# A hybrid SSD and attention block: the attention stage's banks, order and score pipeline rearranged

## The chip, the core and the metric

The kernel runs on one core of one Trainium2 chip. Its time is in device microseconds (us), taken over repeated executions; the profile shows one execution. The engines are TensorE (PE, with its weight loads as PEld), VectorE (DVE), ScalarE (ACT), GpSimd (POOL) and SyncE (SP, which here only starts transfers). Each takes its instructions in the order in which they were written into its queue, and waits where an operand or a buffer is not ready.

## The reference

One layer for 512 tokens of width 2048, float32. An input projection makes everything that two mixers need; an SSD (state space) mixer and an attention mixer give 1024 columns each; an output projection, a norm and a gated feed-forward stage follow.

```python
u = rmsnorm(h, attn_norm_w[l])
z, xbc, dt_raw, q, kc, vc, ks, vs, kw, vw, gate_raw = jnp.split(u @ w_in[l], split_at, axis=-1)
y_ssd = ssd_mixer(z, xbc, dt_raw, ...)       # ends in rmsnorm(y * silu(z), norm_w)
y_att = nsa_mixer(q, kc, vc, ks, vs, kw, vw, gate_raw, ...)
h = h + jnp.concatenate([y_ssd, y_att], axis=-1) @ w_out[l]
v = rmsnorm(h, ffn_norm_w[l])
h = h + (jax.nn.silu(v @ w_gate[l]) * (v @ w_up[l])) @ w_down[l]
return rmsnorm(h, final_norm_w)
```

The attention mixer has 16 heads in four groups of four; a group shares keys and values. Each head has three branches that are added under gates: 31 compressed keys (made from `kc` and `vc` by a small two-layer network), selected blocks of keys (with 512 tokens all eight blocks are selected, so this is causal attention over `ks`, `vs`), and a window of 512 (causal attention over `kw`, `vw`). Queries and keys of the last two are rotated (rope).

## The kernel before, in words

Every float32 product is made of three products of "high" and "low" parts: high by high, high by low, low by high. ACT copies a tile to make its high part (`a_hi`, L118), DVE subtracts to make the low part (`lo`, L121). So every weight tile passes ACT and DVE before PE can use it.

The input projection is cut into 41 **units**. A unit loads 128 output columns of `w_in` in four pieces (`wraw`), splits them (`whi`, `wlo`) and runs 16 k-steps of three matmuls of 512 columns (L241 to L243, in `run_unit`), 48 in all, into one PSUM bank. In order: dt and gates, the SSD inputs, four KC units (the inputs of the compression), Z0 to Z3, and then, group by group, [Z4, Z5 before group 1, Z6 before group 2, Z7 before group 3,] VS, KS, Q0, Q1. After them 16 half units, OS0 to OS15 (24 matmuls each), multiply the SSD half of `w_out`; and 16 more, which the text calls OA, its attention half (L1252 to L1254), with the weight blocks of the later stages. From the seventh unit on all units take turns in two banks, `ps_g`. The other six banks belong to chains: `ps_s` (two: scores), `ps_t` (two: transposes), `ps_v` (products with values), `ps_m` (everything small).

What becomes of a unit's result is its **chain**, a Python generator (`ev_vs`, `ev_ks`, `ev_q`, `ev_z`, `ev_os`, ...). Each `yield n` lets n steps pass. The small class `Sched` holds all chains; `tick` advances them by one step. `run_unit` calls `tick` after every k-step, so that the instructions of the chains are written between the weight matmuls. Where something must be finished first, `run_until` ticks without writing weight matmuls: for a unit, when the chain of the unit but one before has ended (the flag `evac`, set at the end of the whole chain); at `pre_att`, when the compression is done and the pools of the SSD stage can be closed for those of attention; and at others that `wait` for flags.

Chains hold each other up by named holds and single buffers: `ro` (rope's result; a K or Q chain holds it to its end), `qv`, `m` (bank `ps_m`), `fo`. Values are transposed through `ps_m` (L713), keys and queries get rope (two small transfers through POOL's queue, one product on DVE, one on POOL).

The chain `attention` is one generator for all groups. For each group it waits for K, V and both Q of that group, then makes the softmax over the compressed keys (`sc`), transposes it (L864), and only then runs 32 items (four heads, two branches, four query blocks), a new one every second step, through stages: scores on PE (L883, L884), maximum on DVE (L893), exponential on ACT (L900), norm on DVE or ACT (L906, L908), transpose on PE (L926), high part on ACT and low part `ptl` on DVE, and, after a branch's fourth block, eight products with the values on PE (L949). A group's pipeline is run empty before the next group begins.

From VS0 on, each `run_unit` stands under `tc.manual_schedule()`: its instructions are queued as the program wrote them. Elsewhere the library's scheduler is free to reorder instructions between writing and queueing, by its own estimate of their times.

The sum of squares for the SSD norm is kept in `acc2`; its statistics (`rms_stats`, matmuls L292, transposes L302) are made at the beginning of OS0's chain. `ms_hook` loads the eight finished SSD tiles during the last unit of the projection and splits them on ACT and DVE. `stat_s` makes the statistics of the next norm after OS15.

Of the kernel before, what the change touches and what calls it, by code (L numbers as in the profile page):

```python
# [27 lines left out]
EB = 5  # L28
# [80 lines left out]
def body(ctx, tc, xT, w_in, w_out, w_gate, w_up, w_down, w1k, w1v, cols, rows, kst, out):  # L109
# [111 lines left out]

    def run_unit(u):
# [8 lines left out]
        p = p[:, 0:u.cols[1] - u.cols[0]]  # L231
        for i, k0, n in u.sub:
# [89 lines left out]
    def ev_dtg(p):  # L322
# [3 lines left out]
        mul(dve, t, p[0:64, :], rrow[0:64, :])  # L326
        yield 2
# [46 lines left out]
    def conv(t, p):  # L374

        sp = pools["ssd"][1]
        xp = sp.tile([128, 515], F32, tag="xpad", name="xpad", bufs=2)
        dve.memset(xp[:, 0:3], 0.0)
        mul(dve, xp[:, 3:515], p, rrow)
        y = sp.tile([128, 512], F32, tag="c", name="cv", bufs=3)  # L380
# [179 lines left out]
    def ev_z(t):  # L560
        def ev(p):
            yield from sch.wait("r1", ("y", t // 4))
            g, j = divmod(t, 4)
            if g == 0:
                sp = pools["ssd"][1]
                zs = sp.tile([128, 512], F32, tag="zs", name="zs", bufs=2)
                mul(dve, zs, p, rrow)
                act.activation(zs, zs, AF.Silu)
# [4 lines left out]
            else:  # L573
# [6 lines left out]
                mul(dve, zs, p, rrow)  # L580
                yield 1
# [16 lines left out]
    def ev_kc(g):  # L598
        def ev(p):
# [5 lines left out]
            for n, b in (("kc2", 0), ("vc2", 64)):  # L605
                for par in range(2):
                    mul(dve, R[n][par * 64:par * 64 + 64, g, :], p[b:b + 64, par::2], rrow[b:b + 64, par::2])
            if g == 3:
# [92 lines left out]
    def ev_vs(g):  # L701
        def ev(p):
# [4 lines left out]
            mul(dve, t, p, rrow)  # L707
            yield 2
# [39 lines left out]
    def ev_ks(g):  # L748
        def ev(p):
# [4 lines left out]
            mul(dve, t, p, rrow)  # L754
            yield 1
# [32 lines left out]
    def ev_q(g, j):  # L788
        def ev(p):
# [4 lines left out]
            mul(dve, t, p, rrow)  # L794
            yield 1
# [32 lines left out]

    def attention():
        yield from sch.wait("att", "cmp")  # L830
        ap = pools["att"][1]
        vpad = ap.tile([128, 4, 128], F32R, name="vpad")
# [3 lines left out]
        for g in range(4):  # L836
            yield from sch.wait(("k", g), ("v", g), ("q", g, 0), ("q", g, 1))
            kh, kl = R["k", g]
            v = R["v", g]

            sc = R["sc", g]
            sm = ap.tile([128, 3, 4, 4], F32, tag="sm", name="sm", bufs=1)
            dve.tensor_reduce(sm[:, 0], sc, AX.X, ALU.max)
            dve.tensor_scalar(sm[:, 0], sm[:, 0], -1e20, None, op0=ALU.max)
            dve.tensor_tensor(sc.rearrange("p i h k -> p (i h) k"), sc.rearrange("p i h k -> p (i h) k"),
                              sm[:, 0].rearrange("p i h -> p (i h)")[:, :, None].to_broadcast([128, 16, 32]),
                              ALU.subtract)
            yield 1
            act.activation(sc, sc, AF.Exp, scale=0.125)
            for h in range(4):  # L850
                a_hi(vpad[32 * h:32 * h + 32, h, 0:64], vcmp[:, g, :])
            yield 2
            for h in range(4):
                lo(dve, vpad[32 * h:32 * h + 32, h, 64:128], vcmp[:, g, :], vpad[32 * h:32 * h + 32, h, 0:64])
            dve.tensor_reduce(sm[:, 1], sc, AX.X, ALU.add)
            dve.tensor_scalar(sm[:, 1], sm[:, 1], 1e-30, None, op0=ALU.max)
            dve.reciprocal(sm[:, 2], sm[:, 1])
            mul(dve, sm[:, 2], sm[:, 2], gat[:, :, 12 * g:12 * g + 12:3])
            mul(dve, sc.rearrange("p i h k -> p (i h) k"), sc.rearrange("p i h k -> p (i h) k"),
                sm[:, 2].rearrange("p i h -> p (i h)")[:, :, None].to_broadcast([128, 16, 32]))  # L860
            yield 6
            p = ps_t()
            for i in range(4):
                pe.transpose(p[:, i * 128:(i + 1) * 128], sc[:, i].rearrange("p h k -> p (h k)"), ident)  # L864
            sch.flags.add(("sc", g))
            yield 1
            ch = ap.tile([128, 512], F32R, tag="cph", name="cph", bufs=1)
            cl = ap.tile([128, 512], F32R, tag="cpl", name="cpl", bufs=1)
            a_hi(ch, p)
            yield 1  # L870
            lo(dve, cl, p, ch)
            yield 2

            items = [(h, br, i) for h in range(4) for br in range(2) for i in range(4)]
            pt, pr, po = {}, {}, {}

            def score(h, br, i):
                L = 128 * (i + 1)  # L880
                q = R["rq", g, h // 2][:, h % 2, i * 128:(i + 1) * 128]
                p = pr[h, br, i] = ps_s()
                pe.matmul(p[:, 0:L], q, kh[:, br, 0:L], start=True, stop=False)  # L883
                pe.matmul(p[:, 0:L], q, kl[:, br, 0:L], start=False, stop=True)  # L884
                if (br, i) == (1, 3):
                    sch.flags.add(("h", g, h))

            def top(h, br, i):
                L = 128 * (i + 1)
                p = pr[h, br, i]  # L890
                e = ap.tile([128, 512], F32, tag="e", name="e", bufs=EB)
                m = ap.tile([128, 4], F32, tag="em", name="em", bufs=EB + 1)
                dve.tensor_tensor_reduce(e[:, 0:L], p[:, 0:L], kcs(K_AM + 512 - L, L), -0.125, 3e38,  # L893
                                         ALU.add, ALU.min, m[:, 0:1])
                pr[h, br, i] = (e, m)

            def expo(h, br, i):
                L = 128 * (i + 1)
                e, m = pr[h, br, i]
                act.activation(e[:, 0:L], e[:, 0:L], AF.Exp, scale=-1.0, bias=m[:, 0:1], accum_out=m[:, 1:2])  # L900

            def norm(h, br, i):
                L = 128 * (i + 1)
                e, m = pr[h, br, i]
                gc = (4 * g + h) * 3 + 1 + br
                dve.reciprocal(m[:, 2:3], m[:, 1:2])  # L906
                if br:
                    dve.tensor_scalar(e[:, 0:L], e[:, 0:L], m[:, 2:3], gat[:, i, gc:gc + 1],  # L908
                                       op0=ALU.mult, op1=ALU.mult)
                else:  # L910
                    mul(dve, m[:, 3:4], m[:, 2:3], gat[:, i, gc:gc + 1])

            def norm2(h, br, i):
                L = 128 * (i + 1)
                e, m = pr[h, br, i]
                if not br:
                    a_hi(e[:, 0:L], e[:, 0:L], scale=m[:, 3:4])

            def trans(h, br, i):
                e, m = pr[h, br, i]  # L920
                if i == 0:
                    pt[h, br] = (ap.tile([128, 13, 128], F32R, tag="pth", name="pth", bufs=2),
                                 ap.tile([128, 13, 128], F32R, tag="ptl", name="ptl", bufs=2))
                p = ps_t()
                for kb in range(i + 1):
# [963 lines left out]
```

## Time and profile before

| | |
|---|---|
| median of 3 runs | 2312.17 us (2308.17 to 2313.32) |
| span of the profiled execution | 2311.7 us |
| PE busy | 2196.5 us, 95% |
| projection and SSD units, to Z3's end | to about 298 us |
| attention stage, VS0 to the end of OS15 | about 298 to 818 us |
| OA, feed-forward, last norm | from about 827 us |

How to read it: the page gives for the span of one execution the busy time of each engine, and in 40 slices how busy each was, with the clock granted to PE. The page gives no time for what lies around the span. A matmul's row gives its start and a modelled length; since matmuls overlap, the distance between starts tells more than the length. An idle time is put down to the engine whose signal came last. A view by stretches gives the busy time of each engine between two moments, which shows where a stage is dense.

### The profile page before, as it was taken

Reading aid. Unit: us, or ns where it says so; the run is one execution under the profiler, and the core shown is the slowest. Engines: PE = TensorE matmul, PEld = TensorE weight load, DVE = VectorE, ACT = ScalarE, POOL = GpSimd, SP = SyncE. Lnnn points to the kernel's source line nnn. Section 1 sums busy time; section 2 is a strip of 40 time slices with the busy share of each in tenths; the row PEclk is TensorE's granted clock in tenths of the full one; section 3 lists DMA queues with packets and bytes.
Section 4 is the critical chain, followed back from the end, with each engine's and each line's share of the span. In section 5 each row is a group of like instructions: output and inputs, shape, how many; then the busy total and the mean of one; then the engine's idle time right before and its main releaser. Section 6 shows DMA issues by size and latency. Waiting matters only on the chain. (4 is left out here: it accounts for less than half of the span.)

```text
span 2311.7 us, 39742 instructions
## 1 busy us (share of the span) xinstructions
PE 2196.5 (95%) x15376; PEld 2039.8 (88%) x15376; DVE 1809.7 (78%) x2921; ACT 1091.2 (47%) x1768; POOL 422.2 (18%) x435
## 2 busy tenths in 40 slices
PE   7999988989989989999999999999999698989997
PEld 5888877878878878999999999999999698989997
DVE  7799754768788857888888888888888697878786
ACT  4554433757676634544444444444444243333353
POOL 1011214132232134100000000000101121212122
PEclk9999989999999999999999999999999899999998
DMA  5222432221233366787878787887878857677776
GB/s 176 89 74 74 133 110 87 73 72 63 76 101 125 105 198 180 207 233 219 242 217 243 221 249 226 245 227 231 233 219 250 323 170 264 186 254 233 259 162 171
DMA packets 151469, 417.34 MB, mean 181 GB/s; under 512 B 16320, under 2 KB 21968, under 8 KB 151280
## 3 DMA queue, kind: packets, MB, share of 16 engines
q1 hardware_dynamic: 99264, 250.99, 31.5%
q0 software_dynamic: 25456, 76.78, 17.3%
q10 hardware_dynamic: 26560, 87.04, 10.5%
q8 instruction: 120, 1.97, 0.3%
q14 instruction: 69, 0.57, 0.1%
HBM read 353.67 MB, written 57.15 MB: 178 GB/s over the span
## 5 line engine op out<-in xcount | busy, mean ns | idle before, releaser
L118 ACT ACTIVATE R<-Z 128x1024 fp32r<-128x1024 f32 (+4 forms) x488 | 441.5, 922 | 573.0 <-DVE Z L127 320.6
L121 DVE TENSOR_TENSOR R<-Z,R 128x1024 fp32r<-128x1024 f32 (+4 forms) x381 | 392.3, 1035 | 28.5 <-ACT R L118 19.7
L241 PE MATMUL ps_g<-u,whi 128*128 128x512 f32 x720 | 301.1, 418 | 9.5 <-ACT whi L118 9.5
L242 PE MATMUL ps_g<-u,whi 128*128 128x512 f32 x720 | 284.3, 395 | 0.0
L243 PE MATMUL ps_g<-u,wlo 128*128 128x512 f32 x720 | 284.3, 397 | 0.0
L1252 PE MATMUL ps_g<-u,R 128*128 128x256 f32 (+1 forms) x834 | 250.5, 300 | 0.7 <-ACT R L118 0.7
L1253 PE MATMUL ps_g<-u,R 128*128 128x256 f32 (+1 forms) x834 | 249.7, 299 | 0.0
L1254 PE MATMUL ps_g<-u,R 128*128 128x256 f32 (+1 forms) x674 | 200.5, 298 | 0.1
L1252 PE MATMUL ps_t<-u,R 128*128 128x256 f32 x688 | 194.0, 282 | 0.0
L1253 PE MATMUL ps_t<-u,R 128*128 128x256 f32 x688 | 193.9, 282 | 0.0
L1252 PE MATMUL ps_s<-u,R 128*128 128x256 f32 x686 | 193.7, 282 | 0.0
L1253 PE MATMUL ps_s<-u,R 128*128 128x256 f32 x686 | 193.5, 282 | 0.0
L118 ACT ACTIVATE whi<-wraw 128x512 fp32r<-128x512 f32 x196 | 122.4, 626 | 145.2 <-PE ps_g L242 94.6
L121 DVE TENSOR_TENSOR wlo<-wraw,whi 128x512 fp32r<-128x512 f32 x196 | 145.9, 748 | 46.1 <-ACT whi L118 45.4
L241 PEld LDWEIGHTS ps_g<-u,whi 128*128 128x128 f32 x720 | 137.7, 191 | 33.1 <-ACT whi L118 11.4
L1252 PEld LDWEIGHTS ps_g<-u,R 128*128 128x128 f32 x834 | 158.3, 190 | 6.6 <-ACT R L118 0.9
L243 PEld LDWEIGHTS ps_g<-u,wlo 128*128 128x128 f32 x720 | 136.7, 190 | 30.7 <-DVE wlo L121 0.7
L1253 PEld LDWEIGHTS ps_g<-u,R 128*128 128x128 f32 x834 | 158.3, 190 | 5.9
L1254 PE MATMUL ps_s<-u,R 128*128 128x256 f32 x566 | 160.0, 283 | 0.6 <-DVE R L121 0.6
L242 PEld LDWEIGHTS ps_g<-u,whi 128*128 128x128 f32 x720 | 137.7, 191 | 19.7
L121 DVE TENSOR_TENSOR E<-Z,R 128x1024 fp32r<-128x1024 f32 x107 | 130.4, 1218 | 5.6 <-ACT R L118 5.6
L127 DVE TENSOR_TENSOR Z<-Z 128x1024 f32<-128x1024 f32 (+5 forms) x119 | 126.2, 1061 | 8.3 <-POOL Z L127 5.3
(449 smaller groups left out, 6464.3 us busy)
## 6 DMA issues: line engine op xcount, KB each, us to landing
Z<-in_w_gate SPq DMA_DIRECT2D x96, 512.0 KB, 5.3
Z<-in_w_up SPq DMA_DIRECT2D x94, 512.0 KB, 7.3
wraw<-in_w_in SPq DMA_DIRECT2D x164, 256.0 KB, 3.0
g_d<-A ACTq DMA_DIRECT2D x22, 1792.0 KB, 7.1
u<-g_d ACTq DMA_DIRECT2D x12, 1792.0 KB, 16.3
Z<-in_w_gate POOLq DMA_DIRECT2D x37, 512.0 KB, 7.4
Z<-in_w_up POOLq DMA_DIRECT2D x36, 512.0 KB, 5.6
Z<-in_w_down SPq DMA_DIRECT2D x52, 320.0 KB, 5.8
```

What stands on the lines that cost most here:

```text
L118: act.activation(dst, src, AF.Copy, scale=scale)
L121: eng.tensor_tensor(dst, src, f(hi), ALU.subtract)
L127: eng.tensor_tensor(o, a, b, ALU.add)
L241: pe.matmul(p, hi_t[i][:, j, :], ah, start=(k == 0), stop=False)
L242: pe.matmul(p, hi_t[i][:, j, :], al, start=False, stop=False)
L243: pe.matmul(p, lo_t[i][:, j, :], ah, start=False, stop=(k == u.nk - 1))
L1252: pe.matmul(q, h[:, k, :], ah, start=(k == 0), stop=False)
L1253: pe.matmul(q, h[:, k, :], al, start=False, stop=False)
L1254: pe.matmul(q, l[:, k, :], ah, start=False, stop=(k == s.blk.n - 1))
```

## The change

1. The flag `evac` is set by `was_read`, called in each chain right behind the instruction that reads the unit's bank, and no longer at the end of the chain.
2. `tc.manual_schedule()` is gone: the scheduler orders the attention stage too.
3. `attention` no longer goes group by group. The compressed branch of each group is a chain of its own (`compressed`), and one loop carries 128 items over all four groups: an item starts every second step when its group's K, V and Q flags are set. Only the first product of a group waits for that group's compressed branch (`pre`).
4. The units of a group come in the order K, Q0, Q1, V.
5. `pre_att` no longer ticks until the compression is done; a chain (`att_mem`) waits for it and opens the pools, while units go on.
6. The statistics of the SSD norm are a chain of their own (`ssd_norm`), which starts when Z7's chain has ended; the row goes to `acc2`, and the sum of squares of the next norm to `rrow`. The `h1` tiles alternate between the buffers `yz` and `qs`.

```diff
+    def was_read(p):
+        sch.flags.add(("evac", unit_of[id(p)]))
...
             yield from u.evac(p)
-            sch.flags.add(("evac", n_u))
+            assert ("evac", n_u) in sch.flags
...
             mul(dve, t, p, rrow)
+            was_read(p)
             yield 2
             yield from after(("a", g - 2))
...
+    def compressed(g):
+        yield from sch.wait(("q", g, 0), ("q", g, 1))
...
+        if g:
+            yield from sch.wait(("cp", g - 1))
...
+        R["cp", g] = (ch, cl)
+        sch.flags.add(("pre", g))
...
-            for t in range(2 * n + 15):
-                for d in sorted(stages, reverse=True):
-                    if (t - d) % 2 == 0 and 0 <= (t - d) // 2 < n:
-                        stages[d](*items[(t - d) // 2])
-                yield 1
-            sch.flags.add(("a", g))
+        while live or at < len(items):
+            if at < len(items) and t - last >= 2:
+                g = items[at][0]
+                if all(x in sch.flags for x in (("k", g), ("v", g), ("q", g, 0), ("q", g, 1))):
+                    live.append((items[at], t))
+                    last, at = t, at + 1
+            for x, t0 in live:
+                if t - t0 == 11 and x[1:] == (0, 0, 3):
+                    yield from sch.wait(("pre", x[0]))
+                if t - t0 in stages:
+                    stages[t - t0](*x)
...
     def pre_att():
-        sch.run_until("cmp", *[("gy", t) for t in range(4)])
+        sch.add(att_mem())
+
+    def att_mem():
+        yield from sch.wait("cmp", *[("gy", t) for t in range(4)])
...
-        order += [U_Z[t] for t in z] + [U_VS[g], U_KS[g]] + U_Q[g]
+        order += [U_Z[t] for t in z] + [U_KS[g]] + U_Q[g] + [U_VS[g]]
...
+    def ssd_norm():
+        yield from sch.wait(*[("gy", t) for t in range(8)])
+        yield from hold("m")
+        yield from rms_stats(acc2, 1024, acc2, "r2")
+        held.remove("m")
...
-            with tc.manual_schedule():
-                run_unit(u)
+            run_unit(u)
```

Three places in PE's queue show what moves. Lines of the changed kernel have other numbers: L241 to L243 become L247 to L249, L643 to L645 become L655 to L657, L883 and L884 become L902 and L903, L926 becomes L945, L949 becomes L972, L292 and L302 become L299 and L309, L1252 becomes L1295.

The first place is the compression of the values, PE's queue, before: `w1h`, `w1l` are pieces of its first weight, `xh`, `xl` the blocks of tokens, `hd` its hidden layer, `w2vh`, `w2vl` the second weight.

```order
L643 MATMUL ps_s_2774<-w1h_3050,xh_3055 124x256
L644 MATMUL ps_s_2774<-w1l_3051,xh_3055 124x256
L645 MATMUL ps_s_2774<-w1h_3050,xl_3056 124x256
L655 MATMUL ps_t_3108<-ident_77,hd_3080 128x124 x2
L690 MATMUL ps_s_3123<-w2vh_3119,hh_3112 32x64
L691 MATMUL ps_s_3123<-w2vl_3120,hh_3112 32x64
L692 MATMUL ps_s_3123<-w2vh_3119,hl_3113 32x64
```

The same compression after, one piece earlier; `ps_g_3237` is the bank of unit Q0 of group 0, with its weights `whi` and `wlo`.

```order
L655 MATMUL ps_s_2774<-w1h_2976,xh_2981 124x256
L656 MATMUL ps_s_2774<-w1l_2977,xh_2981 124x256
L657 MATMUL ps_s_2774<-w1h_2976,xl_2982 124x256
L248 MATMUL ps_g_3237<-u_94,whi_3238 128x512
L249 MATMUL ps_g_3237<-u_94,wlo_3254 128x512
L247 MATMUL ps_g_3237<-u_94,whi_3238 128x512
L248 MATMUL ps_g_3237<-u_94,whi_3238 128x512
L249 MATMUL ps_g_3237<-u_94,wlo_3254 128x512
L655 MATMUL ps_s_2774<-w1h_3013,xh_3018 124x256
```

Before, the last pieces of the compression follow each other with no weight matmul between; after, weight matmuls of a unit of the attention stage stand between two pieces.

The second place is the SSD norm, PE's queue, before, between OS0 (`ps_g_6804`) and OS1. `kh`, `kl` and `rq` are keys and queries of group 2, `pth`, `ptl` transposed scores, `v` values.

```order
L241 MATMUL ps_g_6804<-u_94,whi_6641 128x512
L242 MATMUL ps_g_6804<-u_94,whi_6641 128x512
L243 MATMUL ps_g_6804<-u_94,wlo_6671 128x512
L883 MATMUL ps_s_6939<-kh_5379,rq_5956 128x512
L884 MATMUL ps_s_6939<-kl_5380,rq_5956 128x512
L292 MATMUL ps_m_6955<-ones_76,acc2_95 128x1 x4
L883 MATMUL ps_s_6966<-kh_5379,rq_5956 128x128
L884 MATMUL ps_s_6966<-kl_5380,rq_5956 128x128
L949 MATMUL ps_v_6844<-pth_6811,v_5020 128x512
```

After, the same four matmuls of the norm, in unit K of group 3 (`ps_g_6014`):

```order
L902 MATMUL ps_s_5631<-kh_4371,rq_4754 128x256
L903 MATMUL ps_s_5631<-kl_4372,rq_4754 128x256
L945 MATMUL ps_t_5555<-ident_77,e_5457 128x128 x4
L945 MATMUL ps_t_5585<-ident_77,e_5492 128x128
L299 MATMUL ps_m_6133<-ones_76,acc2_95 128x1 x4
L247 MATMUL ps_g_6014<-u_94,whi_5962 128x512
L248 MATMUL ps_g_6014<-u_94,whi_5962 128x512
L249 MATMUL ps_g_6014<-u_94,wlo_5989 128x512
```

The norm's matmuls move ahead by four units, from a run of chains into a unit.

The third place is the end of the stage, PE's queue, before: the last weight matmuls of OS15, the statistics of the next norm, the first matmuls of OA (`R` is the high part of an OA weight).

```order
L241 MATMUL ps_g_8373<-u_94,whi_8336 128x512
L242 MATMUL ps_g_8373<-u_94,whi_8336 128x512
L243 MATMUL ps_g_8373<-u_94,wlo_8349 128x512
L292 MATMUL ps_m_8459<-ones_76,acc2_95 128x1 x4
L302 MATMUL ps_m_8472<-ident_77,rst_79 128x128 x4
L1252 MATMUL ps_g_8446<-u_94,R_8420 128x512
```

After, the last rows ahead of OA; 39 rows lie between the last weight matmul of OS15 and L1295.

```order
L309 MATMUL ps_m_8369<-ident_77,rst_79 128x128 x4
L945 MATMUL ps_t_7998<-ident_77,e_7927 128x128 x3
L945 MATMUL ps_t_8018<-ident_77,e_7951 128x128 x4
L972 MATMUL ps_v_7970<-pth_7947,v_7007 128x512
L972 MATMUL ps_v_7970<-ptl_7948,v_7007 128x512
L972 MATMUL ps_v_7970<-pth_7947,v_7007 128x384
L972 MATMUL ps_v_7970<-ptl_7948,v_7007 128x384
L972 MATMUL ps_v_7970<-pth_7947,v_7007 128x256
L972 MATMUL ps_v_7970<-ptl_7948,v_7007 128x256
L972 MATMUL ps_v_7970<-pth_7947,v_7007 128x128
L972 MATMUL ps_v_7970<-ptl_7948,v_7007 128x128
L1295 MATMUL ps_g_8343<-u_94,R_8317 128x512
```

Scores, transposes and products of the last head and a half now stand behind the last weight matmul, with the statistics between them. From OA on, the queues of PE hold the same instructions in the same order as before.

More of the change, by code (lines that the diff above doesn't have):

```diff
@@ L858, in attention @@
[L858 to L865, printed above, removed]
-            yield 1
@@ L867, in attention @@
[L867 to L886, printed above, removed]
@@ L919, in trans @@
[L919 to L925, printed above, removed]
-                    pe.transpose(p[:, kb * 128:(kb + 1) * 128], e[:, kb * 128:(kb + 1) * 128], ident)
-                pr[h, br, i] = p[:, 0:128 * (i + 1)].rearrange("p (a b) -> p a b", b=128)
@@ new lines, in trans @@
+        def trans(g, h, br, i):
+            e, m = pr[g, h, br, i]
+            if i == 0:
+                pt[g, h, br] = (ap.tile([128, 13, 128], F32R, tag="pth", name="pth", bufs=2),
+                             ap.tile([128, 13, 128], F32R, tag="ptl", name="ptl", bufs=2))
+            p = ps_t()
+            for kb in range(i + 1):
+                pe.transpose(p[:, kb * 128:(kb + 1) * 128], e[:, kb * 128:(kb + 1) * 128], ident)
+            pr[g, h, br, i] = p[:, 0:128 * (i + 1)].rearrange("p (a b) -> p a b", b=128)
@@ new lines, in high, with low, pvmm @@
+        def high(g, h, br, i):
+            a_hi(pt[g, h, br][0][:, slice(i, 3 * i + i + 1, 3), :], pr[g, h, br, i])
+        def low(g, h, br, i):
+            th, tl = pt[g, h, br]
+            d = slice(i, 3 * i + i + 1, 3)
+            lo(dve, tl[:, d, :], pr.pop((g, h, br, i)), th[:, d, :])
+        def pvmm(g, h, br, i):
+            if i < 3:
+                return
+            th, tl = pt.pop((g, h, br))
+            if br == 0:
+                o = po[g, h] = ps_v()
+                ch, cl = R["cp", g]
+                vpad = R["vpad"]
+                pe.matmul(o, vpad[:, h, :], ch, start=True, stop=False)
+                pe.matmul(o, vpad[:, h, :], cl, start=False, stop=False)
+                if h == 3:
+                    sch.flags.add(("cp", g))
+            o, v = po[g, h], R["v", g]
+            for kb in range(4):
+                for t in (th, tl):
+                    rhs = t[:, 4 * kb:3 * kb + 4, :].rearrange("p a b -> p (a b)")
+                    pe.matmul(o[:, kb * 128:512], v[:, kb, br, :], rhs, start=False,
+                              stop=(br == 1 and kb == 3 and t is tl))
@@ new lines, in out_c @@
+        def out_c(g, h, br, i):
+            k = 2 * g + h // 2
+            if br == 1 and i == 3 and h % 2 and k > P2["at"]:
+                lo(dve, P2["ma"][k][1], R["at"], P2["ma"][k][0])
+                sch.flags.add(("at", k))
+        items = [(g, h, br, i) for g in range(4) for h in range(4) for br in range(2) for i in range(4)]
+        stages = {0: score, 1: top, 2: expo, 4: norm, 5: norm2, 7: trans, 8: high, 9: low, 11: pvmm, 13: out_a,
+                  14: out_b, 15: out_c}
+        live, t, last, at = [], 0, -2, 0
```

227 lines of the change are left out of this document (119 added, 108 removed).

## The prediction

> **What bounds the kernel now.** I read the page's slices first, then the busy time of each engine by stretches of the attention stage, then who waited for whom on PE, then single rows at the stage's end.
>
> ```profile
> PE 2196.5 (95%) x15376; PEld 2039.8 (88%) x15376; DVE 1809.7 (78%) x2921; ACT 1091.2 (47%) x1768; POOL 422.2 (18%) x435
> ...
> PE   7999988989989989999999999999999698989997
> ...
> PEclk9999989999999999999999999999999899999998
> ```
>
> PE is busy 95% of the span, so the kernel is PE's; but the slices between the sixth and the fifteenth (58 us each) show 8s, and one shows a lowered clock. That is the stage that the change rewrites. The next view cuts it at the places where units of weight matmuls begin and end (columns: us, busy time of PE, of its weight loads, of DVE, ACT and POOL with counts, granted clock, DMA).
>
> ```profile
> core 0: us, PE busy (x) PEld busy (x) DVE busy (x) ACT busy (x) POOL busy (x), PEclk, DMA share, GB/s
> 34.00:298.00 264.00, 264.00 (x1322) 220.90 (x1322) 212.90 (x429) 127.53 (x205) 37.71 (x37) 1.00 0.29 98
> 298.00:334.20 36.20, 27.69 (x161) 22.88 (x159) 19.32 (x45) 15.15 (x36) 7.66 (x13) 0.82 0.25 84
> 334.20:371.30 37.10, 37.10 (x165) 30.77 (x166) 16.17 (x25) 13.92 (x24) 15.29 (x16) 0.94 0.32 103
> 371.30:405.30 34.00, 27.76 (x120) 21.89 (x119) 16.29 (x31) 12.28 (x23) 11.02 (x11) 0.90 0.28 92
> 405.30:481.70 76.40, 75.75 (x412) 63.79 (x411) 61.18 (x185) 56.87 (x142) 18.17 (x20) 1.00 0.21 66
> 481.70:517.60 35.90, 29.60 (x135) 23.89 (x134) 20.02 (x35) 14.88 (x27) 10.97 (x12) 0.90 0.27 84
> ...
> 643.50:668.00 24.50, 22.92 (x132) 19.40 (x132) 23.74 (x62) 21.61 (x50) 9.36 (x9) 1.00 0.42 140
> 668.00:694.60 26.60, 19.55 (x109) 15.94 (x108) 18.32 (x56) 17.29 (x42) 10.37 (x11) 0.92 0.23 75
> 694.60:717.60 23.00, 23.00 (x100) 19.21 (x101) 17.70 (x39) 13.21 (x28) 4.83 (x5) 0.87 0.33 114
> 717.60:798.80 81.20, 80.30 (x423) 66.60 (x422) 73.30 (x202) 54.81 (x143) 16.57 (x18) 1.00 0.38 123
> ...
> 817.90:830.10 12.20, 5.16 (x20) 4.33 (x20) 3.50 (x5) 3.96 (x5) 3.76 (x3) 0.72 0.52 176
> ...
> 298.00:817.90 519.90, 486.70 (x2492) 403.66 (x2490) 376.67 (x977) 312.92 (x733) 142.99 (x156) 0.96 0.28 92
> ```
>
> From 34 to 298 us, the projection and SSD stage, which the library's scheduler already orders, PE is busy all 264.00 us at full clock. From 298 to 817.9 it is idle 33.2 of 519.9 us at a mean clock of 0.96. The loss lies in four places, each followed by a clock below 1.00; the long stretches of attention between them (405 to 482, 718 to 799) lose under 1 us each. Who was late there:
>
> ```profile
> PE ps_g L241 <- ACT whi L118: 9.5, 6, 3.2
> PE ps_m L292 <- DVE acc L127: 4.7, 1, 4.7
> PE ps_t L926 <- DVE ptl L121: 4.4, 4, 2.6
> PE ps_s L643 <- ACT w1h L118: 4.3, 2, 2.3
> PE ps_t L864 <- DVE sc L124: 3.9, 2, 2.0
> ```
>
> These are no engines at their limit (DVE is busy 376.67 of 519.9 us, 72%). They are places where the recording passes scheduler steps without a weight matmul: the program writes down chains (compression, rope, scores) in steps, three weight matmuls a step, and where a unit waits for a bank or for the pools, steps go by bare, so the next weight halves stand behind the chain on ACT and PE has nothing. Counted through the program, 38 steps are bare before; after, only the 5 of the last drain.
>
> **The change part by part.** Instructions on PE and DVE stay the same in number. What moves is worth idle time plus clock. A lowered clock is half speed, so a stretch's (1 - PEclk) times its length, doubled, is its time at half speed; what of that time PE idled costs nothing more, the rest costs half of itself.
>
> *Compression without a stop (L644 loop, the pools' step `pre_att`).* Idle 36.2 - 27.69 = 8.5 us. Clock 0.18 x 36.2 + 0.06 x 37.1 = 8.7 us, so 17.4 us at half speed, some 6 of it idle: 5.7 us. Together 14.2. The units K0 and Q0 now run beside these chains, so I leave 1 us of waits: **13 us**. If this cover failed, all 14.2 would stay.
>
> *Banks given back when read, and keys and queries first.* 371.3 to 405.3: idle 6.2, half speed 6.8 us with 2 of it idle (the wait of L864 for `sc`): 2.4; **8.6 us**. 481.7 to 517.6: idle 6.3, half speed 7.2 us less 2: 2.6; **8.9 us**. The scores of the first group then start in unit Z4, where they now start at the end of Z5, so no group has to be awaited bare. The multiply that frees a bank still stands behind the holds on `ro` and `qv` and, behind it on DVE, the weight lows; that is the second rival below.
>
> *SSD norm early, one pipeline over the groups.* 643.5 to 717.6: idle 1.6 + 7.05, half speed 2 x (0.08 x 26.6 + 0.13 x 23.0) = 10.2 us less 2.6 (the longest wait for `ptl`): 3.8; together 12.4. After, the matmuls of L292 and L302 for the SSD norm stand in unit K3, four units earlier, with weight matmuls on both sides. But DVE was busy 23.74 of 24.5 us just before, with the split of the eight SSD tiles, which stays where it was: I keep 5 and count **7.4 us**.
>
> *The scheduler's order in place of the written one.* The scheduled stretch (34 to 298) shows no idle PE, the written one loses about 1 us in each long stretch: **3 us**, bounded by +20 (small waits inside "busy", which this view hides) and -15 (below).
>
> *The end of the stage.* Weight matmuls run 0.227 us apart (24 in 5.22 us), and then:
>
> ```profile
> 812.46 0.39 PE L241 MATMUL ps_g<-u,whi 128*128 128x512 f32 x1
> ...
> 817.68 0.39 PE L243 MATMUL ps_g<-u,wlo 128*128 128x512 f32 x1
> ...
> 820.11 1.26 POOL L127 TENSOR_TENSOR h<-h,sw 128x512 f32<-128x512 f32 x1 [3.95 <-DVE h L124]
> ...
> 822.81 1.46 PE L292 MATMUL ps_m<-ones,acc 128*128 128x1 f32 x8 [4.74 <-DVE acc L127]
> ...
> 827.33 0.78 PE L1252 MATMUL ps_g<-u,R 128*128 128x512 f32 x1
> ```
>
> Now PE waits 9.65 us here for the sum of squares, at clock 0.72. After, the order leaves the last head and a half of attention behind the last weight matmul. Its chain, by the means of these rows:
>
> ```profile
> L893 DVE CUSTOM_DVE_ANT_0 e<-ps_s,kc 128x128 f32<-128x128 f32 (+3 forms) x128 | 61.8, 482 | 12.4 <-PE ps_s L884 11.4
> L900 ACT ACTIVATE e<-e,em 128x128 f32<-128x128 f32 (+3 forms) x128 | 71.4, 557 | 37.4 <-DVE em L893 23.2 <-DVE em L906 13.6
> L908 DVE TENSOR_SCALAR e<-e,em,gat 128x128 f32<-128x128 f32 (+1 forms) x64 | 39.4, 616 | 2.2
> L118 ACT ACTIVATE pth<-ps_t 128x128 fp32r<-128x128 f32 (+3 forms) x128 | 54.9, 429 | 44.6 <-PE ps_t L926 43.9
> L121 DVE TENSOR_TENSOR ptl<-ps_t,pth 128x128 fp32r<-128x128 f32 (+3 forms) x128 | 62.1, 486 | 27.4 <-ACT pth L118 26.9
> L959 ACT ACTIVATE fo<-ps_v 64x512 f32<-64x512 f32 x16 | 9.5, 593 | 4.2 <-PE ps_v L949 2.9 <-POOL ro L127 1.1
> ```
>
> Maximum 0.48, exponential 0.56, norm 0.62, high 0.43, low 0.49 and copy 0.59 make 3.2 us; scores, transposes and the last products on PE about 2.5; the add and the split of the finished tile about 2 (three of the 0.6 kind); then the first lows of the next weights, about 1: 8.7, and for the last, widest item and DVE's other work between, some 4 more: 13 us. That is 3 to 4 us longer than now, but PE does about 5.5 us of attention in it that stood elsewhere (three sets of eight products, each 2,560 columns at 0.227 us for 512, so 1.1 us, then nine or more transposes and two scores). **0 us**, bounded by -4 (the squares' wait is covered) and +8 (DVE has 17 us of work left behind the last weight low, by the same means).
>
> *Small things.* Two more table loads on ACT, and one more tile of attention that goes through DRAM: hidden, since ACT is busy 312.92 of 519.9 us; if not, 2 to 3 us.
>
> Sum: 13 + 8.6 + 8.9 + 7.4 + 3 + 0 = 41 us. The stages behind keep their order instruction for instruction, so 2311.7 - 41 = 2270.7 for the profiled span. The page gives no time around the span; the three times lie from -3.5 to +1.6 us about it, the median +0.5: **2271 us**.
>
> A second way to the sum, which the first can do without: the Trainium skill, Perfetto Trace Analysis, section Identifying the Most-Contended Engine, holds that matmul busy time is no good measure of headroom and that the share of weight loads is. By it the scheduled stretch has 220.90 / 264.00 = 0.837 and the stage 403.66 us of loads, so 482.4 us at that share, a gain of 37.5 where the busy times give 41. The rows bear the page out so far: the stage's loads stand at 0.776 where its busy PE says 0.936.
>
> **The rivals.**
> *More comes back.* If the small waits inside "busy" go too (the +20 above, and half of what I kept), the gain is 60 to 68: about 2248. For it: weight loads at 0.776. Against: attention's short matmuls were as dense in the good stretches (63.79 / 76.40 = 0.835).
> *The tail grows.* All 17 us of DVE's work serial and the clock at half behind it: +8 to +10 in the tail, and group 3's chains later: a gain of about 22, 2290. For it: the order at the end. Against: its parts overlap on ACT and DVE.
> *Slower: the in-order wait for DVE.* PE's queue now has scores, transposes and products set in front of ready weight matmuls by an estimate. If DVE runs behind it, PE stands at each, as with L926 for `ptl`: 4.4 us in 4 waits, 1.1 each. One such wait at every second of the 128 items is 70 us, less 41: +29, **2341**. It decides from 41 / 1.1 = 37 items. For it: DVE at 23.74 of 24.5 us where PE was worst. Against: DVE needs 376.67 of about 479 us, 79%, and the scheduled stretch ran at 212.90 / 264 = 81% with PE never idle.
> *No change.* The holds on `ro` and `qv` keep the banks as long as before, and the bare steps turn into waits on the chip: 2311. Against: units and chains stand side by side in the order.
> *The clock.* The stretches with banks in rotation have clock 1.00 (34 to 298, 405 to 482). Were the whole stage at the 0.87 of 694.6 to 717.6, 0.09 more than now on some 480 us would be 43 us, and the gain gone: 2313. The Trainium skill, TensorE: Matmul & The Clock Gate, section on a second failure mode (cycling through PSUM banks), describes a kernel whose small idles between groups in rotating banks made the clock swing. By that rule handing banks back sooner risks just this; the rows at 1.00 speak against it here.
>
> **How the numbers follow.** Forecast (2258 to 2284) 0.60; more comes back 0.13; the tail 0.13; slower by waits for DVE 0.08; no change 0.04 and the clock 0.02. That is faster 0.86, same 0.06, slower 0.08, where 0.2% (4.6 us) is about what a measurement of this kernel can tell from no change. The range holds the first three and their bounds: 2244 (68 us back) to 2300 (a gain of 12).
>
> **What would show it.** Right: no idle PE and a clock of 1.00 between unit Z3 and the scores of group 0; about 480 us between the end of Z3 and the last weight matmul plus attention; L292's early matmuls without a wait; DVE near 80%; some 13 us between the last weight matmul and L1252. Wrong, if PE shows many waits of about 1 us for `ptl`, `e` or `pth`, if the clock swings within the stage, or if the end takes 20 us.

## The result, and the profile after

The changed kernel takes **2279.73 us** (median of 4 runs, 2276.95 to 2280.96) against 2311.26 us before on the same chip (2308.17 to 2313.32): a ratio of 0.9861, 95% interval 0.9847 to 0.9876, 31.5 us less. Its profiled span is 2279.2 us against 2311.7. The prediction was 2271, in a range from 2244 to 2300: 41 us less, where 31.5 were measured.

The page of the changed kernel, busy time of PE and the slices of PE and its clock:

```profile
PE 2187.7 (96%) x15376; PEld 2041.0 (90%) x15376; DVE 1809.9 (79%) x2921; ACT 1092.5 (48%) x1770; POOL 433.1 (19%) x436
...
PE   7999999999989899999999999999999798989897
...
PEclk9999999999999899999999999999999899999998
```

Of the 8s of before, those in the sixth, seventh and ninth slice are gone; the twelfth (627 to 684 us) keeps its 8, and the one at the stage's end has come a slice nearer, from the fifteenth to the fourteenth (741 to 798 us). The slice with the lowered clock was the sixth and is now the fourteenth. The attention stage cut at its units, in the changed kernel (columns as in the prediction: us, busy time of each engine with counts, granted clock, DMA):

```profile
298.00:313.90 15.90, 15.90 (x93) 13.82 (x91) 12.02 (x24) 8.72 (x18) 4.02 (x6) 1.00 0.53 173
313.90:345.90 32.00, 30.34 (x166) 25.28 (x165) 17.81 (x38) 14.23 (x35) 15.25 (x20) 0.95 0.35 106
345.90:377.00 31.10, 31.10 (x163) 26.49 (x162) 24.98 (x50) 19.93 (x37) 12.83 (x12) 1.00 0.26 84
377.00:604.00 227.00, 227.00 (x1221) 195.53 (x1220) 172.70 (x469) 152.45 (x358) 69.21 (x75) 1.00 0.24 80
604.00:620.00 16.00, 16.00 (x91) 13.96 (x90) 16.00 (x38) 14.52 (x33) 3.46 (x2) 1.00 0.75 236
620.00:645.00 25.00, 22.27 (x109) 18.44 (x108) 23.48 (x65) 17.17 (x43) 8.30 (x8) 0.92 0.28 94
645.00:671.30 26.30, 25.75 (x123) 20.78 (x123) 20.06 (x54) 16.44 (x40) 5.03 (x5) 0.95 0.28 88
671.30:687.40 16.10, 11.76 (x63) 8.83 (x61) 15.47 (x51) 12.43 (x36) 6.29 (x7) 0.94 0.24 71
...
771.30:790.70 19.40, 12.98 (x64) 10.49 (x62) 8.94 (x22) 8.12 (x18) 2.87 (x3) 0.75 0.52 177
298.00:790.70 492.70, 477.00 (x2505) 404.97 (x2503) 381.47 (x981) 316.15 (x739) 150.50 (x160) 0.98 0.31 101
```

and the same stage of the kernel before, from the same point to its own first matmul of the next stage:

```profile
298.00:827.30 529.30, 489.06 (x2504) 405.78 (x2503) 379.36 (x981) 314.50 (x735) 146.75 (x159) 0.96 0.29 93
```

The stage is 529.3 - 492.7 = 36.6 us shorter, of which 24.5 are idle time of PE (40.2 to 15.7) and 12.1 fewer busy us, at a mean clock of 0.98 for 0.96. One profile of a stage is good to some 3 us: the changed kernel profiled once more (run 10) has the first matmul of its next stage at 787.4 us for 790.7. From 346 to 620 us PE has no idle time at full clock. Of the 15.7 us of idle time that are left, 14.0 lie at two places: where the output units begin (620 to 687 us) and at the stage's end (771 to 791 us). Behind the stage 4 of the 36.6 us are lost again: the last matmul comes 32.9 us earlier, not 36.6.

### The profile page after: what moved, and what is told of

Its sections match the earlier page's. It is cut to its first block, busy times and chain, and to the rows that moved or that the text cites. A ratio compares the mean times of both kernels' runs of the same rounds, so it can differ in the third digit from the quotient of the medians.

```text
span 2279.2 us, 39794 instructions
## 1 busy us (share of the span) xinstructions
PE 2187.7 (96%) x15376; PEld 2041.0 (90%) x15376; DVE 1809.9 (79%) x2921; ACT 1092.5 (48%) x1770; POOL 433.1 (19%) x436
## 5 line engine op out<-in xcount | busy, mean ns | idle before, releaser
L247 PE MATMUL ps_g<-u,whi 128*128 128x512 f32 x720 | 288.4, 401 | 0.3 <-DVE h L124 0.3
L249 PE MATMUL ps_g<-u,wlo 128*128 128x512 f32 x720 | 285.1, 396 | 0.0
L248 PE MATMUL ps_g<-u,whi 128*128 128x512 f32 x720 | 284.4, 395 | 0.0
L1295 PE MATMUL ps_g<-u,R 128*128 128x256 f32 (+1 forms) x834 | 250.7, 301 | 4.3 <-ACT R L118 4.3
L121 DVE TENSOR_TENSOR wlo<-wraw,whi 128x512 fp32r<-128x512 f32 x196 | 152.6, 781 | 61.2 <-ACT whi L118 59.9
L1295 PE MATMUL ps_t<-u,R 128*128 128x256 f32 x688 | 193.8, 282 | 0.0
L1295 PE MATMUL ps_s<-u,R 128*128 128x256 f32 x686 | 193.7, 282 | 0.0
L1295 PEld LDWEIGHTS ps_g<-u,R 128*128 128x128 f32 x834 | 158.3, 190 | 10.2 <-ACT R L118 4.6
L1296 PEld LDWEIGHTS ps_g<-u,R 128*128 128x128 f32 x834 | 158.6, 190 | 5.9
L249 PEld LDWEIGHTS ps_g<-u,wlo 128*128 128x128 f32 x720 | 136.1, 189 | 27.4
L247 PEld LDWEIGHTS ps_g<-u,whi 128*128 128x128 f32 x720 | 136.6, 190 | 25.9 <-DVE h L124 0.9
L1297 PEld LDWEIGHTS ps_g<-u,R 128*128 128x128 f32 x674 | 128.1, 190 | 5.6 <-DVE R L121 1.5
```

The costliest lines, as they stand in the source:

```text
L121: eng.tensor_tensor(dst, src, f(hi), ALU.subtract)
L247: pe.matmul(p, hi_t[i][:, j, :], ah, start=(k == 0), stop=False)
L248: pe.matmul(p, hi_t[i][:, j, :], al, start=False, stop=False)
L249: pe.matmul(p, lo_t[i][:, j, :], ah, start=False, stop=(k == u.nk - 1))
L1295: pe.matmul(q, h[:, k, :], ah, start=(k == 0), stop=False)
L1296: pe.matmul(q, h[:, k, :], al, start=False, stop=False)
```

## The experiments

The prediction gave most of the gain to program steps that pass without a weight matmul ("bare"), and 3 us to the scheduler's order. The first four runs ask whether that division holds: theory A is the prediction's, theory B gives the gain to the scheduler's order. Each run's ratio is to the kernel before, run beside it on the same chip; the changed kernel's are 0.9861 (above) and 0.9857 (run 10).

**1. The written order back.**

```
             if n == len(order) - 1:
                 u.hook = ms_hook
-            run_unit(u)
+            with tc.manual_schedule():
+                run_unit(u)
```

> The changed kernel with one part undone: the units of the attention stage stand in the order in which the program writes them, as before, and not in the scheduler's. Theory A (the time lay in the program's bare steps, 38 before and 5 after; the scheduler's order adds only the 3 us of the prediction's sum): about 2283 us, 3 above the changed kernel's 2279.7; since the written order sets the last heads of attention ahead of the last weight matmuls, the stage's tail falls from 19.4 us to about 10, which may bring it level or below. Theory B (the scheduler's order fills the gaps, bare steps or not): most of the gain of 31.6 us goes, about 2305 us.

Measured: 2323.46 us beside 2314.08, ratio 1.0041 (1.0026 to 1.0056): 42 us slower than the changed kernel, and slower than before, with no bare step but those of the last drain. The longest waits of PE in this run from 298 to 835 us (columns: us in total, times, longest):

```profile
PE ps_g L247 <- ACT whi L118: 8.6, 4, 4.4
PE ps_t L945 <- DVE cpl L121: 4.8, 4, 2.4
PE ps_t L945 <- ACT e L118: 4.5, 7, 1.0
PE ps_g L249 <- DVE wlo L121: 4.3, 5, 1.7
PE ps_s L655 <- ACT w1h L118: 3.8, 4, 1.2
```

and its first stretch and its whole stage:

```profile
298.00:339.80 41.80, 33.34 (x160) 26.71 (x159) 21.30 (x49) 16.53 (x39) 7.74 (x13) 0.71 0.25 80
...
298.00:837.60 539.60, 494.37 (x2505) 408.92 (x2504) 382.81 (x985) 314.82 (x740) 148.19 (x160) 0.95 0.29 93
```

Unit K0 and the compression are now written beside one another, and the stretch loses 8.5 us of PE all the same, at clock 0.71. The bare steps have become waits: PE stands at the chain's rows (L655, L945) and at the weights (L247, L249) in the order in which they were written. Theory A (2283 us) falls; theory B's 2305 was too low as well, since the run is slower than the kernel before, and why it is slower than that isn't shown.

**2. The scheduler's order alone, on the kernel before.**

```
-            with tc.manual_schedule():
-                run_unit(u)
+            run_unit(u)
```

> The kernel before with one part of the change alone: the scheduler orders the attention stage, and all 38 bare steps stay in the program. Theory A: the losses stay where they were, since the scheduler cannot set weights beside a chain whose steps the program has passed without them (what comes later in the program comes later in its estimate too); about 2308 us, 3 below the 2311.3 of before. Theory B: about 2285 us, with the idle PE of 298 to 334 and of 371 to 405 us filled by later weight matmuls.

Measured: 2289.24 us, ratio 0.9896 (0.9879 to 0.9914): one part of six gives 25 us, with all 38 bare steps in the program. How, shows the place of the compression. The kernel before, single rows of PE (start, duration, line, tiles):

```profile
313.95 0.28 PE L645 MATMUL ps_s<-w1h,xl 128*124 128x256 f32 x1
314.27 0.33 PE L676 MATMUL ps_s<-hh,w2h 128*128 128x128 f32 x1
314.75 0.33 PE L677 MATMUL ps_s<-hl,w2h 128*128 128x128 f32 x1
```

and this run:

```profile
314.56 0.28 PE L645 MATMUL ps_s<-w1h,xl 128*124 128x256 f32 x1
314.68 0.40 PE L242 MATMUL ps_g<-u,whi 128*128 128x512 f32 x1
...
319.03 0.23 PE L676 MATMUL ps_s<-hh,w2h 128*128 128x128 f32 x1
319.09 0.44 PE L243 MATMUL ps_g<-u,wlo 128*128 128x512 f32 x1
```

The 4.3 us between two steps of the chain are filled with weight matmuls of the next unit, which the program writes down only after the stop. L241 alone (a third of the weight matmuls) counted from 312.4 to 334.2 us, in the kernel before:

```profile
312.40:334.20 21.80, 0.04 (x1) 0.04 (x1) 0.71 0.17 54
```

and in this run:

```profile
312.40:334.20 21.80, 6.37 (x17) 3.00 (x16) 1.00 0.40 129
```

Seventeen for one. At this place a step that the program passes bare is thus no gap on the chip once the scheduler orders the stage.

**3. Banks given back late.** The flag that a bank is free is set at the end of a unit's chain again.

```
     def was_read(p):
-        sch.flags.add(("evac", unit_of[id(p)]))
+        pass
...
-            assert ("evac", n_u) in sch.flags
+            sch.flags.add(("evac", n_u))
```

> The changed kernel with one part undone: a unit's bank counts as given back at the end of its chain, as before, so that the units after the queries and values wait in the program again (20 bare steps: 3 + 2 in each of the four groups). Theory A: the prediction's terms for this part come back in the places that showed them, 8.6 + 8.9 = 17.5 us, and the 5 steps of the other two groups cost a few us each at the most: 2297 to 2302 us. Theory B: the scheduler fills these steps too, under 3 us: 2280 to 2283 us.

Measured: 2281.83 us, ratio 0.9856 (0.9839 to 0.9874), the changed kernel's. Twenty bare steps cost nothing that can be measured; the prediction had 8.6 + 8.9 us there (with the units' order).

**4 and 11. The SSD norm late.**

```
         sch.flags.add("att")
-        sch.add(ssd_norm())
...
         def ev(p):
+            if c == 0:
+                yield from ssd_norm()
             yield from sch.wait("r2", "x")
```

> The changed kernel with one part undone: the matmuls and the statistics of the SSD norm stand in the first output unit again and not in unit K3. No bare step comes back by it. Theory A by steps alone: the same time, 2280 us within 3. Theory A by the prediction's term for this part: up to 7.4 us more, 2287 us, if the wait of 4.7 us for the sum of squares and the clock behind it come back at the output units. If the crowding of DVE between 620 and 687 us is what costs there, moving the norm into it adds 2 to 5 us: 2282 to 2285.

Measured: 2275.87 us, ratio 0.9833 (0.9813 to 0.9853), faster than the changed kernel. That was neither theory's, so the kernel ran again beside the changed one, in more rounds:

> The changed kernel with the SSD norm in the first output unit again, as in the fourth run, to settle its sign beside the changed kernel on the same chip. If the early norm costs, as the 2275.9 us of that run say: 3 to 5 us less than the changed kernel. If that was noise: within 2 us of it.

Measured: 2276.71 us, ratio 0.9849 (0.9834 to 0.9864), beside 2278.36 and 0.9857 (0.9843 to 0.9872) of the changed kernel. The early norm does not help; whether it costs 2 to 4 us stays open, since the intervals overlap.

**5. Values first again.**

```
-        order += [U_Z[t] for t in z] + [U_KS[g]] + U_Q[g] + [U_VS[g]]
+        order += [U_Z[t] for t in z] + [U_VS[g], U_KS[g]] + U_Q[g]
...
-    first_att = U_KS[0]
+    first_att = U_VS[0]
```

> The changed kernel with one part undone: each group's value unit stands ahead of its key and query units again, and the pools' step stands ahead of the first value unit; no bare step comes back. Theory C (formed after the first four runs: the scheduler's order by itself carries about 27 of the 37 us at the stage's end, and where the program has bare steps no longer matters): the order of the units is nothing to a scheduler that takes what is ready, so 2280 us within 3. Theory D (what the scheduler's order alone did not give, 9.8 us at the stage's end, comes from keys and queries first, since group 0's scores then start some 16 us earlier): 2285 to 2290 us.

Measured: 2284.62 us, ratio 0.9891 (0.9877 to 0.9906): 0.3%, some 7 us, slower, with no bare step. The order of the units counts under the scheduler too, and theory C falls. Theory D's time came to within 1 us, but the first scores start 9.6 us later than in the changed kernel (374.2 for 364.6) and not 16, and runs 9 and 5 side by side (below, under run 12) speak against their start as the reason.

**6. The stop at the pools' step.**

```
     def pre_att():
-        sch.add(att_mem())
-
-    def att_mem():
-        yield from sch.wait("cmp", *[("gy", t) for t in range(4)])
+        sch.run_until("cmp", *[("gy", t) for t in range(4)])
         close_pool("cmp")
```

> The changed kernel with one part undone: the program stops at the pools' step until the compression's chain is written down (10 bare steps), as before. The prediction's term for it was 13 us. Theory C: 2280 to 2283 us, as with the 20 bare steps of the late banks (2281.8). Theory D for this part (the 9.8 us left over lie here): 2287 to 2293 us.

Measured: 2280.33 us, ratio 0.9867 (0.9853 to 0.9882), the changed kernel's within 2 us. The prediction had 13 us there.

**7. VectorE relieved where the output units begin.** The eight low halves of the SSD tiles are not made.

```
-            P2["ms"] = [(U[:, 0, i], U[:, 1, i]) for i in range(8)]
+            P2["ms"] = [(U[:, 0, i], U[:, 0, i]) for i in range(8)]
...
-        k -= 1
-        if 0 <= k < 8:
-            dve.scalar_tensor_tensor(U[:, 1, k], f(U[:, 1, k]), col(C_SN + k), f(U[:, 0, k]), op0=ALU.mult,
-                                     op1=ALU.subtract)
```

> The changed kernel without the eight VectorE instructions that make the low halves of the SSD tiles (0.67 us each, 5.4 us together, at 605 to 625 us); the output units multiply by the high half twice in their place, so the output projection lacks the low part of its SSD half. Theory: PE's idle time between 620 and 687 us is VectorE's, which is behind there (busy 23.5 of 25.0 us, 620 to 645), so the stage ends up to 5.4 us earlier: 2274 to 2277 us. Rival: the hole is latency of the chain from the loads of those tiles to their products, or PE's fixed order behind the scores: 2279 to 2281 us.

Measured: 2275.53 us, ratio 0.9849 (0.9832 to 0.9865). The median lies where the theory had it, but the interval reaches to the changed kernel's 0.9857 and 0.9861, so the time doesn't tell the two apart. The windows of its profile:

```profile
604.00:620.00 16.00, 16.00 (x92) 13.98 (x91) 10.89 (x31) 13.69 (x31) 2.92 (x2) 1.00 0.67 216
620.00:645.00 25.00, 20.96 (x105) 17.10 (x104) 23.30 (x59) 16.82 (x42) 8.44 (x8) 0.97 0.32 107
...
671.30:687.40 16.10, 11.85 (x56) 8.72 (x55) 15.16 (x45) 12.35 (x35) 6.24 (x6) 0.89 0.24 73
```

VectorE has 5.1 us less to do from 604 to 620 us (10.89 for 16.00), and PE's idle time behind it is no smaller: 4.0 us from 620 to 645 (2.7 in the changed kernel) and 4.25 from 671 to 687 (4.3). That speaks for the rival. But the profiled execution took 2283.24 us, and the other three, of which there is no profile, 2274.84 to 2276.12. Whether the split of the SSD tiles costs time there stays open, within the 5.4 us of the theory.

**8. The last output units in the written order.**

```
-            run_unit(u)
+            if n >= len(order) + 6:
+                with tc.manual_schedule():
+                    run_unit(u)
+            else:
+                run_unit(u)
```

> The changed kernel with the written order for output units 6 to 14 alone, and the scheduler's for all ahead of them. Theory: the 19.4 us between the last weight matmul of the stage and the next stage's first (13.0 busy, at clock 0.75) come from the scheduler's taking weights early and leaving the last head and a half of attention alone at the end; in the written order weights stand beside all of attention, the tail falls to about 10 us, and the stage ends 5 to 9 us earlier: 2271 to 2275 us. Rival: in the written order PE stands about 1 us at each chain's row again, as in the run with the written order throughout, and what the tail gives is lost there: 2280 to 2287 us.

Measured: 2282.79 us, ratio 0.9882 (0.9868 to 0.9897), some 5 us slower than the changed kernel, at the edge of the intervals. Attention now ends well ahead of the last weights (last product at 755.1 us, last weight matmul at 785.4, next stage at 795.3), so the tail is 9.9 us for 19.4; what it gives, the written order takes back ahead of it: output unit 6 alone lasts 32.4 us there (7.2 in the changed kernel).

**9. Two parts alone.** The kernel before, with the scheduler's order as in run 2 and the order keys, queries, values as the changed kernel has it; the stop, the late banks, the late norm and the four pipelines stay.

```
-        order += [U_Z[t] for t in z] + [U_VS[g], U_KS[g]] + U_Q[g]
+        order += [U_Z[t] for t in z] + [U_KS[g]] + U_Q[g] + [U_VS[g]]
...
-            with tc.manual_schedule():
-                run_unit(u)
+            run_unit(u)
```

> The kernel before with two parts of the change alone: the scheduler orders the stage, and each group's units stand in the order keys, queries, values; all the bare steps stay (40 with this order), and so do the late banks, the stop, the late SSD norm and the four separate pipelines. Theory E (formed after eight runs: attention, from group 0's first score to the last product, takes 404 to 423 us in every kernel so far and ends the stage, so what counts is when group 0's first score starts: 404.2 us before, 380.8 with the scheduler alone, 364.6 in the changed kernel, 374.2 in it with values first): keys first bring the first score some 10 us nearer, 2281 to 2284 us. Rival: without the single pipeline and the compression in a task of its own this order is worth nothing, 2288 to 2290 us, as with the scheduler alone.

Measured: 2278.36 us, ratio 0.9861 (0.9840 to 0.9882). Its stage, from 298 us to the next stage's first matmul:

```profile
298.00:790.50 492.50, 476.18 (x2504) 404.09 (x2502) 375.18 (x980) 317.51 (x739) 147.80 (x160) 0.98 0.31 101
```

That is the changed kernel's stage (492.70 us, 477.00 busy) without four of its six parts, and with 32 bare steps in the program (the 40 of the expectation were a miscount). The time is below theory E's 2281 to 2284 us and far from its rival's 2288 to 2290, though the first score starts at 375.1 us, 5.7 ahead of run 2's, where theory E looked for some 10. The other four parts together are worth nothing that these intervals (0.2% to either side) can show; the single pipeline was not undone by itself.

**10. The changed kernel again**, as the yardstick beside runs 9, 11 and 12.

> The changed kernel itself, as the yardstick for the two runs beside it: 2279.7 us within 2, a ratio to before of 0.986 to 0.987.

Measured: 2278.36 us (2275.91 to 2279.51), ratio 0.9857 (0.9843 to 0.9872).

**12. Gate units later**, on the kernel of run 11.

```
-        z = {0: [], 1: [4, 5], 2: [6], 3: [7]}[g]
+        z = {0: [], 1: [], 2: [4, 5], 3: [6, 7]}[g]
```

> The changed kernel with the SSD norm late and with the gate units Z4 and Z5 after group 1's units and Z6 and Z7 after group 2's, so that group 1's keys, queries and values come 32 program steps earlier and its scores can follow group 0's without the 13.5 us between them (458.5 to 472.1 us in the changed kernel). Theory E: attention gets shorter by about that, and the stage ends 8 to 14 us earlier than with the norm late alone: 2262 to 2268 us. Rival: VectorE (381 of 493 us in this stage) has no room for groups closer together, or the weights that the scheduler takes early only run out sooner: within 4 us of the norm late alone, 2272 to 2280 us.

Measured: 2281.88 us, ratio 0.9870 (0.9855 to 0.9884), 5 us more than run 11, just above the rival's range too. Group 1's scores follow group 0's after 8.0 us for 13.6 (they start at 467.9, in run 11 at 470.4), but the last product comes at 790.2 (782.6 in run 11). Theory E falls as far as it says that attention's own length ends the stage; run 8, where the last product comes 40 us ahead of the next stage, says the same, and so do runs 9 and 5: their first scores start at 375.1 and 374.2 us, and their times lie 6 us apart. Nor is the length of attention the 404 to 423 us of theory E: the traces give 392.3 in run 8 and 426.6 in run 3.

## Why the prediction was right, and where its steps were wrong

The time was forecast from where the loss lay, and that held: the stage was to come back to about the density of the scheduled stretch, and it did. From 298 us to the last weight matmul the share of weight loads is (404.97 - 10.49) / 473.3 = 0.833 after, against 0.776 before and the 0.837 that the second way took. But the terms were given to the wrong parts. That their sum, 41 us, lies within 10 of the 31.5 measured is luck as far as its parts go: most of what the wrong parts were to give came from the one that was put at 3 us. The second way's 37.5 us beside the 36.6 that the stage gained are luck in part too. Its stage ends at 817.9 us, ahead of the wait at the end; to the next stage's first matmul (405.78 us of loads in 529.3) the same share would have given 44 us, and the end, with loads for 10.49 of 19.4 us, kept most of the rest.

- **The step that failed** is the one that named the cause: "They are places where the recording passes scheduler steps without a weight matmul", 38 before and 5 after. Runs 2, 3, 6 and 9 have 38, 20, 10 and 32 bare steps under the scheduler's order, and at 2278 to 2289 us most or all of the gain is there all the same; run 1 has none, in the written order, and is 42 us slower than the changed kernel. The bare steps were a property of the program, and were taken for one of the queues. The rival *no change* had described it: in the written order the bare steps turn into waits on the chip.
- **The scheduler's order** was sized at 3 us, with +20 as the bound. By itself it gives 25 (run 2), above the bound; taken away it costs 42 (run 1). The first window that the prediction shows spoke for it (34 to 298 us, scheduled, no idle PE); it was applied only to the stretches that already ran well, not to the four places that did not.
- **Compression without a stop**, 13 us: the place gave 12.7 (the unit behind the first four starts at 358.6 us for 371.3), but by the scheduler: with its order alone that unit starts at 357.0 (run 2), and with the stop alone put back nothing is lost (run 6).
- **Banks given back and keys first**, 17.5 us: the banks give nothing (run 3); the order of the units gives about 7 (run 5), and together with the scheduler's order all that the change gives (run 9).
- **SSD norm early**, 7.4 us with the one pipeline: nothing, perhaps a loss of 2 to 4 (runs 4 and 11). The 5 us that were kept for VectorE's crowding were too few: the idle time from 620 to 687 us is 2.73 + 0.55 + 4.34 = 7.6 us, beside a clock of 0.92 to 0.95. Whether the reason given, the split of the SSD tiles, has a part in it stays open (run 7). PE's longest waits in the changed kernel, from 298 to 800 us:

```profile
PE ps_s L902 <- DVE em L912: 5.2, 6, 2.0
PE ps_g L1295 <- ACT R L118: 3.5, 1, 3.5
PE ps_v L972 <- ACT pth L118: 1.7, 3, 0.7
```

  The scores wait for a bank that VectorE's maximum has yet to read; all six waits lie between 620 and 687 us. Output unit 5 starts 16.1 us after unit 4's last matmul, and only attention's rows stand between, though eleven output units are still to come. What unit 5 lacks, until 686.75 us, is a bank of `ps_g`. Rows of VectorE that read such banks, with the first matmuls of units 4 and 5 and one row of GpSimd:

```profile
664.24 0.67 DVE L124 TENSOR_TENSOR h<-ps_g,acc 128x512 f32<-128x512 f32 x1
664.96 0.51 PE L247 MATMUL ps_g<-u,whi 128*128 128x512 f32 x1 [0.30 <-DVE h L124]
...
680.67 1.29 POOL L127 TENSOR_TENSOR h<-h,sw 128x512 f32<-128x512 f32 x1 [1.43 <-DMA sw<-in_xT]
...
686.08 0.67 DVE L124 TENSOR_TENSOR h<-ps_g,acc 128x512 f32<-128x512 f32 x1
687.36 0.78 PE L247 MATMUL ps_g<-u,whi 128*128 128x512 f32 x1
```

  By the order of VectorE's queue the row at 664.24 reads unit 3's bank and the one at 686.08 unit 2's, 32.7 us after unit 2's last matmul; unit 5 takes over this bank. Unit 2's result goes to the buffer `yz`, which still holds unit 0's. Unit 0's waits for the tile of the layer's input that is added to it (the row of GpSimd), and this tile is loaded into `sw`, which rope uses for group 3's last queries until 677.9 us. By this reading one small buffer with two uses holds up the weights. It comes from the trace and the program; no run took it apart. With the norm late (run 11) the pause behind unit 4 is 1.7 us, but there is one of 18.0 us between units 0 and 1.
- **The stage's end**, 13 us: 19.4, close to the 20 that the prediction named as a sign of being wrong. The mechanism was right (the last head and a half behind the last weights), the size wasn't. The end of it, rows of PE in the changed kernel:

```profile
771.26 0.39 PE L249 MATMUL ps_g<-u,wlo 128*128 128x512 f32 x1
...
778.93 0.79 PE L972 MATMUL ps_v<-pth,v 128*128 128x512 f32 x1 [0.47 <-ACT pth L118]
...
786.93 0.27 PE L972 MATMUL ps_v<-ptl,v 128*128 128x128 f32 x1
790.70 0.80 PE L1295 MATMUL ps_g<-u,R 128*128 128x512 f32 x1 [3.50 <-ACT R L118]
```

  The mean clock is 0.75 there. Where it is lowered, a product of 512 columns takes 0.79 us for the 0.39 that such a matmul takes at full clock: PE is busy 12.98 us, not the 5.5 of the sum, and idle 6.4. The last 3.5 us are the chain behind the last product, over ACT and VectorE; its rows on ACT:

```profile
787.24 0.59 ACT L982 ACTIVATE fo<-ps_v 64x512 f32<-64x512 f32 x1 [2.07 <-PE ps_v L972]
788.59 0.63 ACT L118 ACTIVATE u<-at 128x512 fp32r<-128x512 f32 x1 [0.76 <-DVE at L127]
...
789.60 2.94 ACT L118 ACTIVATE R<-Z 128x1024 fp32r<-128x1024 f32 x3
```

  Run 8 halves this end, and the time doesn't fall; but its written order loses time ahead of the end, so what a shorter end alone is worth isn't shown.
- **The rival of PE's in-order waits for VectorE** did not come: scores, transposes and products wait for VectorE's and ACT's chains 14 times in the stage, 8.7 us in all (6 of them, 5.2 us, are the scores above), where it decided from 37 waits.
- **Not foreseen**: the 4 us given back behind the stage, with the same instructions in the same order. The runs' next stages differ by as much (from its first matmul to the last 1471.2 us before, 1474.9 after, 1475.3 in the changed kernel again, 1472.3 in run 9); no run followed it.

What stays open: why keys first is worth 7 us under the scheduler's order, since the start of the first scores doesn't explain it (run 12 above); whether the early norm costs; whether the split of the SSD tiles does; and what freeing unit 2's bank sooner would give.

## What to carry to other kernels

A total can come out right from terms that belong to another part: size the loss by place, then ask of each place which part of the change would fill it with all the others absent. Where a scheduler orders a stage, pauses in the recording are not gaps in the queue, and smoothing them by hand may be worth nothing (here two of six parts gave all that could be measured); in a written order, taking the pauses away leaves the waits behind them. Run the scheduler's order alone first.

## What the runs showed of the hardware

VectorE's smallest operations sometimes take several times their length while GpSimd works. In the changed kernel the multiply of one column (`em<-em,gat`) runs 64 times: 53 times it takes at most 0.16 us, and 11 times 0.62 to 1.57, some 9.5 us more in all. Rows of VectorE:

```profile
646.20 0.92 DVE L124 TENSOR_TENSOR em<-em,gat 128x1 f32<-128x1 f32 x1
...
686.74 0.14 DVE L124 TENSOR_TENSOR em<-em,gat 128x1 f32<-128x1 f32 x1
```

and of GpSimd, at the time of the first:

```profile
645.82 1.28 POOL L127 TENSOR_TENSOR h<-h,hx 128x512 f32<-128x512 f32 x1 [8.39 <-issue]
```

The first multiply takes 0.92 us for 0.14 and ends with GpSimd's addition, at 647.1 us. So do all 11: each ends within 0.03 us of the end of a GpSimd operation. The Trainium skill, SBUF — State Buffer, section SBUF: two separate sides, says that the two engines share a port pair of SBUF, the on-chip memory, that the one that starts first holds for a whole instruction, also against a VectorE operation with two SBUF inputs where GpSimd's reads SBUF. The rows agree: in 10 of the 11 GpSimd began first. The other, at 687.11 us, has VectorE begin 0.25 us before GpSimd. No run here took GpSimd's work away to price it.
